# GpSimd left out of the weight splits and the decay products, with another set of thread ranks, in a two-model float32 forward pass

## The chip, the cores and the metric

The kernel runs on one core of one Trainium2 chip. The metric is the time of one execution in microseconds, as the device measures it; lower is better. The engines are named as in the profile: PE (TensorE), DVE (VectorE), ACT (ScalarE), POOL (GpSimd), SP (which issues the DMAs).

## The reference, cut to what matters

256 tokens of width 1024 go through three layers, in float32. Each layer mixes tokens, adds the result to the residual, and runs a gated feed-forward network of width 2816. The three mixers are a linear attention with per-channel decay (and attention over a memory of 256 tokens), a sparse attention in blocks (compressed, selected and windowed keys, and the memory again), and an attention with forget gates beside a pooling branch, with 16 meta tokens ahead of the sequence. The linear attention is the part of which the argument speaks most:

```python
b = jnp.cumsum(gc, axis=2)
o_inter = jnp.einsum('bhtd,bhde->bhte', qc * jnp.exp(b), S)
decay = jnp.exp(jnp.where(causal, b[:, :, :, None, :] - b[:, :, None, :, :], -jnp.inf))
attn = jnp.einsum('bhtd,bhsd,bhtsd->bhts', qc, kc, decay)
o = o_inter + jnp.einsum('bhts,bhse->bhte', attn, vc)
```

The weights are 149 MB in float32 and are read once.

## The kernel before, in words

**Products.** Every large product is made of three TensorE products of rounded parts: the weight is split into `whi` (rounded, made on ScalarE in `_cuts`) and `wlo` (the rest, a subtraction in `_rest`), the activation into `xh` and `xl`, and `mm3` issues hi by hi, lo by hi and hi by lo into one bank of PSUM (`acc`, four of them). One such triple of 128x256 is called a dense triple here. Weights come in chunks of 1 MB into two buffers `wraw`; a chunk is two pieces of 1024 columns, and each piece is one cast to `whi` and one subtraction to `wlo`, 280 pieces in all. A buffer is loaded again when both subtractions of its chunk are done.

**Small work.** Everything else uses four further banks (`att`): scores, transposes, the small products of the three mixers, and the sums for the norms.

**The linear attention.** `expo` makes, for each half `tt` of the tokens and each pair of heads `f`, the tile of exponentials `ge` (8 spans of 128), multiplies it by the queries into `gqe`, and then in place by the keys (128x896 each: these are the decays of the title). At the last span it makes `gkx` or `gqx`, which link the two halves. `levels` then issues, for each half, the products `gqe` by `ge` for spans of 16, 8, 4, 2 and 1 tokens (level 2 to 6, shape 32x16), the diagonal `gq` by `gk` (level 7, 32x32), the two widest spans (64x64 and 32x32), and after both halves `gqx` by `gkx`. `near_pairs` takes the levels out of the banks with predicated copies into `near`, two for each level, and copies `near` into the attention matrix `gat`. `out_rows` multiplies `gat` with the values `gv`. Meanwhile the program's main thread issues dense triples.

**What sets the order.** The kernel is written as threads (generators) that each yield the next operation. `Sched.run` plans with estimated durations and picks the next operation among all threads; the order in which it picks is the order in which the instructions stand in each engine's queue. Of the operations that could start, it takes the one with the lowest sum of estimated start and rank:

```python
                cost, it = min(((self.cost(th, o), o) for o in it.alts), key=lambda c: c[0] + c[1].dur)
                rank = th.prio if it.eng != "P" or th.prio != 9 or self.credit >= 0 else -12
                rank = cost + NEAR * rank
```

The ranks are in the table `PRIO`, by the thread's name. An operation may have alternatives on several engines (written with `|`), of which the planner takes the one with the earliest estimated end. `credit` is an account of how dense TensorE's work has been; when it falls below zero, the main thread's dense triples go first. `RATIO` says how much a dense stretch adds to it, and `LIMIT` is its ceiling. The waits between engines follow from the order in which the instructions were picked: an instruction that touches a tile waits for those before it, in the order of picking, that touched the same part of it in a way that conflicts.

Nearly every instruction of ScalarE, VectorE and GpSimd carries line 335 in the profile, the place where a picked operation is issued, and the matmuls line 516; tiles tell them apart.

Of the kernel before, what the change touches and what calls it, by code (L numbers as in the profile page):

```python
# [153 lines left out]
class Thread:  # L154
    def __init__(self, gen, prio, t, n):
# [2 lines left out]

LNEXP, EXPTANH, SILU = "natural_log_exp_and_others", "exp_and_others", "silu_and_others"
TABLES = {"Exp": (LNEXP, EXPTANH), "Ln": (LNEXP,), "Silu": (SILU,), "Tanh": (EXPTANH,)}  # L160
LOAD, TICK, RATIO, LIMIT, WARM, SWITCH = 1.3, 3.4133, 1.4792, 0.7664, 12, 0.13
NEAR = 0.00100

PRIO = {"_cuts": -18.58, "_load": 1.02, "_loads": -36.85, "_rest": -3.82, "add_residual": -13.55,
        "both_norms": -19.45, "ck_load": -13.23, "ck_loads": -83.76, "coefs": 59.38, "compress": -19.77,
        "consts": 24.44, "decay": -37.28, "evacuate": 6.42, "expo": -55.79, "few_loads": 48.21, "forget": -38.18,
        "fox_chain": -4.22, "fox_pair": 5.05, "proj_few": 10.05, "fox_head": 2.42, "gains": 32.58, "gate": 23.42,
        "gating": -11.27, "head_norm": -20.5, "heads_of": -2.08, "hidden": 7.95, "late_loads": -16.69,
        "levels": 7.47, "mem_chain": -63.57, "mem_head": -11.75, "meta_probs": 1.9, "meta_rows": 0.62,
        "meta_values": -15.47, "mix": -47.97, "near_pairs": -10.15, "nsa_chain": -4.61, "out_rows": -68.21,  # L170
        "output": -6.62, "pads": 18.74, "pooling": -11.72, "rows_done": 28.61, "rstd_rows": -52.41,
        "scale_few": -6.07, "scale_out": -25.81, "scale_tok": -70.73, "selection": 91.16, "silu": 15.66,
        "smalls": 30.82, "square_sum": -6.06, "squares": 39.11, "stack_k": -9.03, "stack_q": 22.34, "swap": 33.71,
        "tile_parts": -14.4, "up": -47.17, "values": -19.21, "warm": -9.83, ("square_sum", 3): 31.92,
        ("square_sum", 5): 13.26}
HOP = {"P": 0.24, "V": 0.14, "S": 0.16, "G": 0.29, "D": 0.24}


# [222 lines left out]
class Weights:  # L401


    def __init__(self, sch, plan, dram, dma, V, S, G, raw, hi, lo):
        self.sch, self.plan, self.dram, self.dma, self.V, self.S, self.G = sch, plan, dram, dma, V, S, G
        self.raw, self.hi, self.lo = raw, hi, lo
        self.chunks, tiles = [], [[] for _ in plan]
        for n, ts in _chunks(plan):
            parts = [Piece() for _ in range(0, n, PIECE)]
            for i, _, o, m in ts:  # L410
                parts[o // PIECE].uses += 1
                tiles[i].append((parts[o // PIECE], o % PIECE, m))
            self.chunks.append((n, parts, Ev()))
        self.blocks = list(zip(plan, tiles))[::-1]
# [38 lines left out]

    def _rest(self, p, raw, o, m, left):
        p.lo = yield self.lo
        parts = p.lo[:, :m], raw[:, o:o + m], p.hi[:, :m].bitcast(FT)
        yield self.V.tensor_sub(*parts) | self.G.tensor_sub(*parts)
        self.sch.set(p.ev)
        left[0] -= 1
        if not left[0]:  # L460
            self.sch.give(self.raw, raw)
# [21 lines left out]
def body(tc, io):  # L483
# [40 lines left out]
    def tr(*calls):  # L524

        def fn():
            for o, a, b in calls:
# [12 lines left out]
    m0 = mem.rearrange("p a b -> p (a b)")  # L540
    gfn, rmeta = base.tile([128, KD], FT, name="gfn"), base.tile([16, 1], FT, name="rmeta")
    tinys = [base.tile([128, 32], FT, name=f"tiny{i}") for i in range(2)]
    W = Weights(sch, _plan(), io["w"], dma, V, S, G, slots(base, 2, [128, CHUNK], "wraw"),
                slots(base, NP, [128, PIECE], "whi", FR), slots(base, NP, [128, PIECE], "wlo", FR))
    rco = base.tile([128, 10], FT, name="rco")
    rsq = base.tile([128, 10], FT, name="rsq")
# [419 lines left out]
    def main():  # L966
# [25 lines left out]
        with ExitStack() as stack:  # L992
# [84 lines left out]
            def expo(tt, f, out):  # L1077
                c = slice(tt * 128, tt * 128 + 128)
                yield la_ev, gr_ev
                et = yield e_  # L1080
                e = et.rearrange("p (a b) -> p a b", a=8)
                qe = yield qes
                for half in range(2):
                    bank = yield att
                    a0 = 128 * tt + 512 * half
                    yield pe(*[(bank, w[:, tt, f * 128:f * 128 + 128], gr[:, a0:a0 + 512], i == 0, i == 1)
                               for i, w in enumerate((lh, ll))])
                    yield S.activation(et[:, half * 512:half * 512 + 512], bank, AF.Exp, scale=1.0 / 16.0)
                    give(att, bank)
                yield q_ev[f], k_ev[f]  # L1090
                l0 = 1 - tt
                yield V.tensor_mul(qe, e[:, l0:l0 + 7], qT[:, f, None, c].to_broadcast([128, 7, 128]))
                ke = e[:, l0:l0 + 7]
                parts = ke, ke, kT[:, f, None, c].to_broadcast([128, 7, 128])
                yield V.tensor_mul(*parts) | G.tensor_mul(*parts)
                if tt == 0:
                    yield V.tensor_mul(kx[:, f, :], e[:, 0], kT[:, f, c])
                else:
                    yield V.tensor_mul(qx[:, f, :], e[:, 7], qT[:, f, c])
                kx_ev[tt, f] = Ev()  # L1100
                sch.set(kx_ev[tt, f])
                out.append((et, qe, ke))
# [973 lines left out]
```

## Time and profile before

| | before |
|---|---|
| three timed runs | 923.35, 929.02, 929.19 us |
| median | 929.02 us |
| the profiled execution | 923.24 us, its span 921.5 us |
| busy, PE / DVE / ACT / POOL | 899.9 / 717.0 / 493.2 / 90.4 us |
| mean granted TensorE clock | 0.989 |

The profiled execution is one more execution beside the timed runs. Its span goes from the first to the last instruction. Matmuls overlap each other in the records, so the distance between the starts of two says more than the duration of one.

### The profile page before, as it was taken

The page shows a single profiled execution, that of the slowest core. Times are in us where ns is not written, and L with a number is a line of the kernel's source. Part 1 is how long each engine was busy: PE and PEld are TensorE (multiplying, and loading weights), DVE is VectorE, ACT ScalarE, POOL GpSimd, SP SyncE. Part 2 cuts the span into 40 slices and gives each one's busy share as a digit, 9 for nine tenths or more (in the row PEclk, how much of TensorE's full clock was granted, in tenths as well). Part 3 has the DMA queues.
Part 4 walks back from the last instruction along what each step waited for, and adds up shares of the span by engine and source line. Part 5 has one row for each costly group of instructions (what it writes and reads, how often), then busy time and mean ns, then how long its engine had stood idle before and what let it go on. Part 6 is the DMA issues. An engine that isn't in the chain of part 4 may idle for free.

```text
span 921.5 us, 19560 instructions
## 1 busy us (share of the span) xinstructions
PE 899.9 (98%) x7967; PEld 864.7 (94%) x7967; DVE 717.0 (78%) x1492; ACT 493.2 (54%) x854; POOL 90.4 (10%) x116
## 2 busy tenths in 40 slices
PE   8988999999999999999999999999999999999998
PEld 7877999999999996989999999999889999999998
DVE  7776588999987687986899999867688777777552
ACT  5644556555554544875565555545666554444431
POOL 3211001000000012300200000112352100000000
PEclk9977999999999999999999999999999999999999
DMA  7721535555555566233445555555323355555651
GB/s 268 265 70 70 183 138 169 198 183 193 200 202 184 190 239 238 90 138 96 180 184 186 200 206 188 184 186 206 131 93 128 127 182 205 185 187 194 217 209 64
DMA packets 26668, 160.19 MB, mean 174 GB/s; under 512 B 3242, under 2 KB 5674, under 8 KB 8530
## 3 DMA queue, kind: packets, MB, share of 16 engines
q1 hardware_dynamic: 26578, 158.94, 48.5%
q8 instruction: 63, 1.03, 0.4%
q14 instruction: 27, 0.22, 0.1%
HBM read 157.62 MB, written 1.05 MB: 172 GB/s over the span
## 4 chain that ended last, share of the span: by engine, by line
PE 86%; DVE 10%; DMA 2%; issue 1%; ACT 0%; SPq 0%; DVEq 0%; ACTq 0%
PE acc L516 76%; PE att L516 8%; DVE wlo L335 4%; PE att L528 2%; DVE xl L335 2%; DMA ck<-in_w_cv_dram 1%; DVE x L335 1%; DVE sum L335 1%; DMA ck<-in_w_ck_dram 1%; DMA mem<-in_w_dram 0%; DVE xh L335 0%; DVE gqx L335 0%; DVE ge L335 0%; DVE gqe L335 0%; DVE near L335 0%
## 5 line engine op out<-in xcount | busy, mean ns | idle before, releaser
L335 ACT CAST whi<-wraw 128x1024 fp32r<-128x1024 f32 x280 | 294.4, 1052 | 319.5 <-PE acc L516 305.0
L335 DVE TENSOR_TENSOR wlo<-wraw,whi 128x1024 fp32r<-128x1024 f32 x279 | 345.2, 1238 | 103.8 <-ACT whi L335 102.9
L516 PE MATMUL acc<-xh,whi 128*128 128x256 f32 (+1 forms) x1440 | 408.2, 283 | 0.1
L516 PE MATMUL acc<-xh,wlo 128*128 128x256 f32 (+1 forms) x1440 | 400.9, 278 | 2.0 <-DVE wlo L335 2.0
L516 PE MATMUL acc<-xl,whi 128*128 128x256 f32 (+1 forms) x1440 | 401.0, 278 | 1.4 <-DVE xl L335 1.3
L516 PEld LDWEIGHTS acc<-xh,whi 128*128 128x128 f32 x1440 | 271.4, 189 | 6.5 <-issue 4.2
L516 PEld LDWEIGHTS acc<-xl,whi 128*128 128x128 f32 x1440 | 271.9, 189 | 2.6 <-DVE xl L335 2.2
L516 PEld LDWEIGHTS acc<-xh,wlo 128*128 128x128 f32 x1440 | 271.4, 188 | 2.8 <-DVE wlo L335 2.8
L516 PE MATMUL acc<-hh,whi 128*128 128x256 f32 x528 | 146.0, 276 | 0.0
L516 PE MATMUL acc<-hl,whi 128*128 128x256 f32 x528 | 145.7, 276 | 0.0
L516 PE MATMUL acc<-hh,wlo 128*128 128x256 f32 x528 | 145.7, 276 | 0.0
L516 PEld LDWEIGHTS acc<-hh,whi 128*128 128x128 f32 x528 | 99.1, 188 | 0.0
L516 PEld LDWEIGHTS acc<-hl,whi 128*128 128x128 f32 x528 | 99.1, 188 | 0.0
L516 PEld LDWEIGHTS acc<-hh,wlo 128*128 128x128 f32 x528 | 99.1, 188 | 0.0
L335 POOL TENSOR_TENSOR sum<-sum,sqt 128x256 f32<-128x256 f32 x27 | 28.9, 1070 | 477.5 <-ACT sqt L335 469.0
L516 PE MATMUL acc<-ch,whi 128*128 128x256 f32 x192 | 55.3, 288 | 0.0
L516 PE MATMUL acc<-cl,whi 128*128 128x256 f32 x192 | 53.1, 277 | 0.0
L516 PE MATMUL acc<-ch,wlo 128*128 128x256 f32 x192 | 53.1, 277 | 0.0
L335 DVE SCALAR_TENSOR_TENSOR fa<-pad,vec,fa 128x256 f32<-128x256 f32 x88 | 41.7, 478 | 0.0
L335 DVE TENSOR_TENSOR fb<-acc,nb 128x256 f32<-128x256 f32 x66 | 28.0, 424 | 12.4 <-PE acc L516 9.6
L516 PEld LDWEIGHTS acc<-ch,whi 128*128 128x128 f32 x192 | 36.1, 188 | 0.7 <-issue 0.4
L335 DVE TENSOR_TENSOR x<-acc,x 128x256 f32<-128x256 f32 x64 | 26.3, 418 | 12.9 <-PE acc L516 12.6
(337 smaller groups left out, 1044.5 us busy)
## 6 DMA issues: line engine op xcount, KB each, us to landing
wraw<-in_w_dram SPq DMA_DIRECT2D x140, 1024.0 KB, 4.8
ck<-in_w_ck_dram SPq DMA_DIRECT2D x4, 512.0 KB, 5.6
ck<-in_w_cv_dram SPq DMA_DIRECT2D x4, 512.0 KB, 5.5
x<-in_x_dram SPq DMA_DIRECT2D x4, 256.0 KB, 6.0
mem<-in_w_dram SPq DMA_DIRECT2D x4, 256.0 KB, 4.6
mem<-in_mem_dram SPq DMA_DIRECT2D x1, 1024.0 KB, 6.9
out_dram<-sqt SPq DMA_DIRECT2D x8, 128.0 KB, 2.1
ge<-in_gcst_dram SPq DMA_DIRECT2D x2, 288.0 KB, 7.5
```

What stands on the lines that cost most here:

```text
L335: op_ = Op(self.name, d, lambda: f(out, *a, **k), table=table)
L516: r = P.matmul(o, a, b, start=s, stop=e)
L528: r = P.transpose(o, a, b)
```

## The change

Two lines lose their alternative on GpSimd: the subtraction to `wlo` and the product of the exponentials with the keys. GpSimd keeps small operations (sums of squares, powers, bias tiles, scalings of 128x128 and the like). All ranks of `PRIO` are other numbers, as are `RATIO`, `LIMIT` and `NEAR`. What is computed is the same. Cut to its core:

```diff
-LOAD, TICK, RATIO, LIMIT, WARM, SWITCH = 1.3, 3.4133, 1.4792, 0.7664, 12, 0.13
-NEAR = 0.00100
+LOAD, TICK, RATIO, LIMIT, WARM, SWITCH = 1.3, 3.4133, 1.3862, 1.2333, 12, 0.13
+NEAR = 0.00101
...
-PRIO = {"_cuts": -18.58, "_load": 1.02, "_loads": -36.85, "_rest": -3.82, "add_residual": -13.55,
+PRIO = {"_cuts": -12.17, "_load": 1.37, "_loads": -52.68, "_rest": -5.17, "add_residual": -7.56,
...
-        parts = p.lo[:, :m], raw[:, o:o + m], p.hi[:, :m].bitcast(FT)
-        yield self.V.tensor_sub(*parts) | self.G.tensor_sub(*parts)
+        yield self.V.tensor_sub(p.lo[:, :m], raw[:, o:o + m], p.hi[:, :m].bitcast(FT))
...
-                parts = ke, ke, kT[:, f, None, c].to_broadcast([128, 7, 128])
-                yield V.tensor_mul(*parts) | G.tensor_mul(*parts)
+                yield V.tensor_mul(ke, ke, kT[:, f, None, c].to_broadcast([128, 7, 128]))
```

What this does to the instructions is seen in the order that the planner made, with and without the change. On TensorE the order is the same through the three feed-forward networks; it differs in the linear attention from the first half's level 5 on, in the sparse attention, and in the third mixer. Of the 280 subtractions to `wlo`, GpSimd has one before and none now, and the products with the keys stand on VectorE before and now. Of the scalings of `np` (the sparse attention's probabilities), GpSimd has two of 128x128 and one of 128x256 before, and five of 128x128 now.

On GpSimd, in the linear attention, before (`nt` and `tiny` are the powers for the norms):

```order
L335 TENSOR_TENSOR sum_90<-sum_90,sqt_86 128x256
L335 TENSOR_TENSOR nt_94<-tiny_64,mhalf 128x2
L335 TENSOR_TENSOR wlo_72<-wraw_66,whi_68 128x1024
L335 TENSOR_TENSOR tiny_98<-tiny_98,mhalf 128x4
L335 TENSOR_TENSOR tiny_99<-tiny_99,mhalf 128x4
```

And now:

```order
L335 TENSOR_TENSOR sum_90<-sum_90,sqt_87 128x256
L335 TENSOR_TENSOR sum_90<-sum_90,sqt_88 128x256
L335 TENSOR_TENSOR sum_90<-sum_90,sqt_86 128x256
L335 TENSOR_TENSOR nt_94<-tiny_64,mhalf 128x2
L335 TENSOR_TENSOR tiny_98<-tiny_98,mhalf 128x4
L335 TENSOR_TENSOR tiny_99<-tiny_99,mhalf 128x4
```

The subtraction is gone, and its neighbours stand as they did.

On VectorE, in the second half of the linear attention, before (from the link `gqx`; `sr` and `mq` are scaled projections, `xl` are the low parts of the memory's activations, `near` the predicated copies):

```order
L335 TENSOR_TENSOR gqx<-ge_132,gq 128x128
L335 TENSOR_TENSOR sr<-acc_113,nb_93 128x256
L335 SCALAR_TENSOR_TENSOR xl_81<-mem,vec,xh_80 128x256
L335 SCALAR_TENSOR_TENSOR mq<-acc_114,nb_93 128x256
L335 SCALAR_TENSOR_TENSOR xl_81<-mem,vec,xh_80 128x256 x7
L335 COPY_PREDICATED near<-gc,att_117 128x2x16
L335 COPY_PREDICATED near<-gc,att_116 128x2x16
L335 TENSOR_TENSOR wlo_73<-wraw_65,whi_69 128x1024
L335 COPY_PREDICATED near<-gc,att_117 128x4x8
L335 COPY_PREDICATED near<-gc,att_116 128x4x8
```

And now:

```order
L335 TENSOR_TENSOR gqx<-ge_132,gq 128x128
L335 TENSOR_TENSOR sr<-acc_113,nb_93 128x256
L335 SCALAR_TENSOR_TENSOR mq<-acc_114,nb_93 128x256
L335 SCALAR_TENSOR_TENSOR xl_81<-mem,vec,xh_80 128x256 x8
L335 TENSOR_TENSOR wlo_72<-wraw_66,whi_68 128x1024
L335 TENSOR_TENSOR wlo_73<-wraw_65,whi_69 128x1024
L335 COPY_PREDICATED near<-gc,att_119 128x2x16
L335 COPY_PREDICATED near<-gc,att_116 128x2x16
```

Two subtractions to `wlo` now stand ahead of the first predicated copy, where one stood between the first pair and the second.

On TensorE, in the same half, with the engines that each waits for, before (16 products of level 7 `gq` by `gk`, of which the first two stand here, then the widest spans):

```order
L516 MATMUL acc3_115<-xh0_78,wlo3_74 128x256
L516 MATMUL att1_117<-gq_135,gk_136 32x32 [waits DVE_49]
L516 MATMUL att0_116<-gq_135,gk_136 32x32
...
L516 MATMUL att1_117<-gqe0_343,ge1_133 64x64 [waits DVE_49]
L516 MATMUL att0_116<-gqe0_343,ge1_133 64x64 [waits DVE_49]
L516 MATMUL att1_117<-gqe1_344,ge0_132 64x64 [waits DMAHW0_49]
```

And now:

```order
L515 MATMUL acc3_115<-xh0_78,wlo3_74 128x256
L515 MATMUL att3_119<-gq_135,gk_136 32x32
L515 MATMUL att0_116<-gq_135,gk_136 32x32
...
L515 MATMUL att3_119<-gqe0_343,ge1_133 64x64
L515 MATMUL att0_116<-gqe0_343,ge1_133 64x64
L515 MATMUL att3_119<-gqe1_344,ge0_132 64x64 [waits DMAHW0_49]
```

The products stand without a wait for VectorE now, since the predicated copies were picked after all of them. The first wait for VectorE that is left in this half for a result of the predicated copies stands later, at the product of `gat` with `gv` for the second half, after nine dense matmuls, the four products of the first half and nine dense matmuls more. In the first half, level 5 waited for the first predicated copy of level 4 and now waits for the two of level 2; a dense triple that stood ahead of it stands behind it.

In the third mixer, for one pair of heads, the sums `hns1` for the head norms, two products `fk` by `fq` and the transposes of `fp3` and `fp0` now stand on TensorE with no dense triple between them, with four waits for VectorE and one for ScalarE; before, a dense triple stood between the sums and the products, one transpose stood behind them, and of the four waits two were for VectorE and two for ScalarE.

The count of places on TensorE where one matmul's tile shape (rows by columns of the array) differs from the next one's is 22 before and 17 now in the linear attention, 34 and 32 in the sparse attention, 56 and 53 in the third mixer.

## Rows read from the trace of the kernel before

**Rows 1.** Windows: busy us (count) of PE, PEld, DVE, ACT, POOL, granted clock, DMA share, GB/s.

```profile
44.40:54.60 10.20, 7.41 (x225) 6.04 (x226) 6.83 (x21) 2.50 (x6) 1.91 (x2) 0.75 0.36 130
54.60:64.80 10.20, 10.20 (x103) 9.34 (x104) 7.46 (x19) 5.86 (x13) 1.77 (x1) 0.75 0.00 0
64.80:75.10 10.30, 5.18 (x229) 4.31 (x219) 8.40 (x26) 2.33 (x6) 1.47 (x1) 0.75 0.29 105
75.10:127.00 51.90, 51.90 (x356) 48.45 (x355) 34.16 (x74) 30.39 (x69) 2.92 (x2) 0.95 0.35 122
...
150.80:327.00 176.20, 176.20 (x1557) 176.20 (x1556) 147.82 (x254) 94.27 (x130) 1.47 (x2) 1.00 0.54 193
327.00:370.00 43.00, 39.94 (x346) 33.47 (x345) 35.53 (x80) 19.74 (x32) 8.35 (x10) 1.00 0.69 241
370.00:460.70 90.70, 89.74 (x744) 82.19 (x743) 73.23 (x231) 61.63 (x160) 12.42 (x15) 1.00 0.34 123
...
638.00:718.00 80.00, 79.20 (x691) 71.12 (x692) 61.08 (x211) 50.86 (x121) 30.04 (x49) 1.00 0.33 119
```

**Rows 2.** Waits of PE for one tile, whole span: total us, times, longest us.

```profile
PE att L516 <- DVE near L335: 7.9, 4, 4.1
```

**Rows 3.** Timeline of PE, first half of the linear attention: start, duration, idle before.

```profile
44.38 0.28 PE L516 MATMUL acc<-xh,wlo 128*128 128x256 f32 x1
44.58 1.07 PE L516 MATMUL att<-gqe,ge 64*32 64x16 f32 x96
...
48.14 0.39 PE L516 MATMUL att<-gqe,ge 64*32 64x16 f32 x32 [1.94 <-DVE near L335]
...
49.94 0.58 PE L516 MATMUL att<-gqe,ge 64*32 64x16 f32 x32 [0.85 <-DVE near L335]
```

**Rows 4.** Timeline of PE, second half, to the last of its products.

```profile
64.63 1.07 PE L516 MATMUL att<-gqe,ge 64*32 64x16 f32 x96
...
72.06 0.52 PE L516 MATMUL att<-gq,gk 64*32 64x32 f32 x32 [4.10 <-DVE near L335]
73.60 1.18 PE L516 MATMUL att<-gqe,ge 64*64 64x64 f32 x24 [1.02 <-DVE near L335]
...
76.24 0.41 PE L516 MATMUL acc<-xl,whi 128*128 128x256 f32 x1
...
81.28 0.37 PE L516 MATMUL acc<-xh,whi 128*128 128x256 f32 x1
```

**Rows 5.** Timeline of DVE over both halves, and in the sparse attention.

```profile
36.52 0.28 DVE L335 TENSOR_TENSOR gkx<-ge,gk 128x128 f32<-128x128 f32 x1
...
63.95 2.67 DVE L335 TENSOR_TENSOR gqx<-ge,gq 128x128 f32<-128x128 f32 x2
66.65 0.42 DVE L335 TENSOR_TENSOR sr<-acc,nb 128x256 f32<-128x256 f32 x1
...
67.72 2.85 DVE L335 SCALAR_TENSOR_TENSOR xl<-mem,vec,xh 128x256 fp32r<-128x256 f32 x7
70.49 0.28 DVE L335 COPY_PREDICATED near<-gc,att 128x32 f32<-128x32 uint8 x2
70.69 1.22 DVE L335 TENSOR_TENSOR wlo<-wraw,whi 128x1024 fp32r<-128x1024 f32 x1
...
75.08 1.22 DVE L335 COPY gat<-near 32x64 f32<-32x64 f32 x8
76.32 0.65 DVE L335 COPY gat<-att 64x128 f32<-64x128 f32 x3
...
385.37 0.37 DVE L335 TENSOR_SCALAR np<-np,tiny 128x128 f32<-128x128 f32 x1
...
387.25 0.28 DVE L335 TENSOR_SCALAR np<-np,tiny 128x128 f32<-128x128 f32 x1
```

**Rows 6.** Timeline of POOL.

```profile
63.03 3.24 POOL L335 TENSOR_TENSOR wlo<-wraw,whi 128x1024 fp32r<-128x1024 f32 x1 [10.59 <-ACT whi L335]
...
385.30 0.60 POOL L335 TENSOR_SCALAR np<-np,tiny 128x128 f32<-128x128 f32 x1 [10.45 <-DVE tiny L335]
```

More of the change, by code (lines that the diff above doesn't have):

```diff
@@ L160 @@
 TABLES = {"Exp": (LNEXP, EXPTANH), "Ln": (LNEXP,), "Silu": (SILU,), "Tanh": (EXPTANH,)}
-LOAD, TICK, RATIO, LIMIT, WARM, SWITCH = 1.3, 3.4133, 1.4792, 0.7664, 12, 0.13
-NEAR = 0.00100
-PRIO = {"_cuts": -18.58, "_load": 1.02, "_loads": -36.85, "_rest": -3.82, "add_residual": -13.55,
[L165 to L175, printed above, removed]
@@ new lines @@
+LOAD, TICK, RATIO, LIMIT, WARM, SWITCH = 1.3, 3.4133, 1.3862, 1.2333, 12, 0.13
+NEAR = 0.00101
+PRIO = {"_cuts": -12.17, "_load": 1.37, "_loads": -52.68, "_rest": -5.17, "add_residual": -7.56,
+        "both_norms": -33.22, "ck_load": -15.44, "ck_loads": -83.53, "coefs": 40.79, "compress": -19.2,
+        "consts": 36.87, "decay": -34.57, "evacuate": 4.06, "expo": -64.07, "few_loads": 45.42, "forget": -21.91,
+        "fox_chain": -3.12, "fox_pair": -7.57, "proj_few": 19.88, "fox_head": 8.36, "gains": 38.33, "gate": 50.08,
+        "gating": -14.29, "head_norm": -36.58, "heads_of": -11.63, "hidden": -0.76, "late_loads": -3.72,
+        "levels": 0.78, "mem_chain": -69.93, "mem_head": -9.86, "meta_probs": -21.08, "meta_rows": -15.24,
+        "meta_values": 4.27, "mix": -62.03, "near_pairs": 2.77, "nsa_chain": -9.52, "out_rows": -71.71,
+        "output": -17.96, "pads": 9.38, "pooling": -17.95, "rows_done": 25.04, "rstd_rows": -64.13,
+        "scale_few": -10.36, "scale_out": -20.17, "scale_tok": -36.67, "selection": 77.08, "silu": 5.66,
+        "smalls": 40.36, "square_sum": -10.21, "squares": 50.38, "stack_k": -3.54, "stack_q": 16.96, "swap": 48.72,
+        "tile_parts": -15.56, "up": -32.71, "values": -13.07, "warm": -5.76, ("square_sum", 3): 28.89,
+        ("square_sum", 5): 15.72}
@@ L401, with __init__ @@
 class Weights:
-    def __init__(self, sch, plan, dram, dma, V, S, G, raw, hi, lo):
-        self.sch, self.plan, self.dram, self.dma, self.V, self.S, self.G = sch, plan, dram, dma, V, S, G
+    def __init__(self, sch, plan, dram, dma, V, S, raw, hi, lo):
+        self.sch, self.plan, self.dram, self.dma, self.V, self.S = sch, plan, dram, dma, V, S
         self.raw, self.hi, self.lo = raw, hi, lo
@@ L542, in body @@
     tinys = [base.tile([128, 32], FT, name=f"tiny{i}") for i in range(2)]
-    W = Weights(sch, _plan(), io["w"], dma, V, S, G, slots(base, 2, [128, CHUNK], "wraw"),
+    W = Weights(sch, _plan(), io["w"], dma, V, S, slots(base, 2, [128, CHUNK], "wraw"),
                 slots(base, NP, [128, PIECE], "whi", FR), slots(base, NP, [128, PIECE], "wlo", FR))
```

## The prediction

> **What bounds the kernel now.** I read the windows first, then TensorE's waits, then the timelines at the places where those waits stand. TensorE is busy for 899.9 of 921.5 us, so time can only come from its idle stretches, from its slow stretches, and from matmuls that take less. In a feed-forward network it is busy without a gap: 1557 dense matmuls in 176.20 us, 0.113 us each, at full clock [rows 1]. The change leaves TensorE's order there as it was, and about 530 us of the span lie in such stretches; I count them at nothing. The sparse attention idles for 3.06 us in its first 43.00 us and 0.96 in the next 90.70, the third mixer for 0.80 of 80.00 [rows 1]: little is to be had there. What is left is the linear attention. From 44.4 to 75.1 us the granted clock is 0.75, half of the time at the lower level, 1.2 GHz instead of 2.4, and in the next 51.9 us it is 0.95 [rows 1]; a dense matmul takes 0.41 us at 76.24 where it takes 0.28 at 44.38 [rows 3, 4]. There TensorE also waits four times for the predicated copies `near`, 7.9 us in all, the longest 4.1 [rows 2]: 1.94 and 0.85 in the first half [rows 3], 4.10 and 1.02 in the second [rows 4].
>
> **The GpSimd alternatives themselves.** Only one subtraction of 280 moves, and no decay product does. On GpSimd it took 3.24 us [rows 6]; on VectorE one takes 1.22 [rows 5]. In its time, from 63.03 on, VectorE's two products `gqx` took 2.67 us, where one of the same shape, the counterpart `gkx` at 36.52, took 0.28 [rows 5]. So VectorE loses 2.67 less 0.56, 2.1 us, beside the subtraction, and 1.22 by taking it over. By themselves these edits are worth at most 0.9 us, and only as far as TensorE waits for VectorE.
>
> **Second half of the linear attention.** Before, from the first level product at 64.63 to the dense matmul behind the last `gv` product at 81.28 are 16.65 us, of which 5.12 are the two waits [rows 4]. The levels stood behind copies that VectorE reached late: `gqx` took 2.67, and from 66.65 to 70.49 came `sr`, `mq` and eight `xl`, 3.84 us, then a subtraction of 1.22 between the copies [rows 5]. Now the products carry no wait for VectorE; the wait has moved to the product of `gat` and `gv`, behind nine dense matmuls, four products and nine dense matmuls. Does VectorE get there in time? From 63.95: two `gqx` at 0.28, 0.56; `sr` to `xl`, 3.84; two subtractions at 1.22, 2.44; twelve predicated copies at 0.14, 1.68; eight `gat` from `near`, 1.22; three from the bank, 0.65 [rows 5]. The sum is 10.39, which ends at 74.3. TensorE has 16.65 less 5.12, 11.53 us of work in the stretch, and three dense triples more, nine matmuls at 0.113, 1.0 us: it would be through at 77.2 without a wait, and the second half's `gv` products, which need `gat`, are the last of it; 2.9 us are left for them behind VectorE's end. So I hold the waits to be gone. Where they go, those three triples come out of later work, so the gain is up to 5.12 us. It is less if the lower clock lasts as long as before and is now spent on dense matmuls: at half speed 5.12 us of waits turn into 5.12 us of work worth 2.56 at full speed. Between 2.56 and 5.12 I take 4.0. Below 2.56 lies a late VectorE: each microsecond beyond the 2.9 us of slack (74.3 against 77.2) costs one, and the second subtraction can itself wait for ScalarE's `whi`, on which nothing here has a price. I let that reach to a gain of nothing.
>
> **First half.** Level 5 now waits for two copies of level 2 instead of one of level 4, and one triple that stood ahead of it stands behind it. The waits are 1.94 and 0.85 [rows 3], so the gain lies between 2.79 and, if the missing triple (0.34 us) is added to the wait, -0.3. With the earlier copy and the later triple pulling opposite ways I take half, 1.4.
>
> **Tile shapes.** From a dense matmul at 44.38 to products of another shape at 44.58 are 0.20 us [rows 3], against 0.113 in a dense run [rows 1]: about 0.09 for a change of shape. There are ten fewer (22, 34 and 56 become 17, 32 and 53), 0.9 us. It is nothing if the change hides under weight loads.
>
> **Sparse attention and third mixer.** All 4.8 us of idle there are the most that could go, and some of it waits for DMAs that the change doesn't touch. Against that, the third mixer has a stretch with five waits and no dense triple between them. Every further wait is new; from a gain of 1 to a loss of 3 I take a loss of 0.5. GpSimd also gets five scalings of `np` of 128x128 for two and a wider one. At 385.30 such a scaling took 0.60 us [rows 6], and VectorE's own beside it 0.37, against 0.28 at 387.25 [rows 5]: 0.09 lost for each, 0.3 for three more, on an engine with slack; it is inside the 0.5. The Trainium skill, SBUF — State Buffer (two separate sides), would make that dearer: the port pair that GpSimd and VectorE share is an exclusive lock, and the loser fully blocks. By that rule three more scalings could hold VectorE for up to 1.8 us instead of 0.3, an estimate from the row's 0.60; this row shows a slowing and no full block, and I keep the row's price.
>
> **Sum.** 923.24 - 4.0 - 1.4 - 0.9 + 0.5 = 917.4 us, against the profiled execution. That execution lies with the fastest of the three timed runs (923.35); the other two are 5.9 us longer, so their median is 929.02. The trace doesn't show what they had more; a further stretch at the lower clock would fit, but that is an inference. I forecast a time like the profiled one's.
>
> **The rivals.**
>
> *The clock stays up.* If TensorE no longer idles in the second half, the clock may not fall there. Before, it was 0.95 over the 51.9 us from 75.1 [rows 1], 5.2 us at half speed, which cost 2.6; with all of the 5.12 gained instead of 4.0 this gives 917.4 - 2.6 - 1.1 = 913.7. For it: the lower clock stands around the waits. Against: the window from 54.6 to 64.8 is at 0.75 too, with TensorE busy for all of its 10.20 us [rows 1], so a busy engine is not at once a fast one. The Trainium skill, TensorE: Matmul & The Clock Gate (What's actually happening), speaks for this rival: the default state is throttled, and activity releases it. The row of the busy window neither confirms nor refutes it.
>
> *The runs keep their longer time.* Whatever lengthened two of three runs by 5.9 us stays, and the median falls among such runs: 917.4 + 5.9 = 923.3. Against it: a stretch with fewer waits has fewer occasions.
>
> *What is gained is given back.* The linear attention's gap moves to the `gat` products, or later small products come late by as much. Then the kernel takes what it took, 923 to 929; I take 924. For it: VectorE's own work grows by 10 instructions and ScalarE's falls by as many, and both feed the same products.
>
> *Slower.* The third mixer's stretch with five waits makes TensorE idle as the linear attention does, and the clock falls with it. The price is the linear attention's own: some 4 us of idle, half of the 7.9 [rows 2], and a stretch like that from 44.4 to 75.1, where half of 30.7 us at half speed cost 7.7 [rows 1], 11.7 together. With only 2.56 and 0.9 gained elsewhere that is 923.24 + 11.7 - 3.5 = 931.4. It decides from the point where those waits and their clock cost more than the 6.3 us that I add up as gains. Against it: before, the third mixer had waits of the same kinds and idled for 0.80 us at a clock of 1.00 [rows 1].
>
> **How the numbers follow.** A measurement of this kernel can tell about 1% from no change, so faster means below 919.7 and slower above 938.3. The forecast has 0.45, of which 0.40 lies below 919.7; the clock that stays up 0.13; the longer runs 0.22; nothing gained 0.10; slower than before 0.10, of which half passes 938.3 if the runs' 5.9 us come on top. Faster is 0.40 + 0.13 = 0.53, slower 0.05, the same the remaining 0.42. The forecast's own range is 914.5 to 920.5. The whole range reaches down to 911, the clock that stays up with the first half's waits gone too, and up to 926, past the longer runs and most of nothing gained; the slower rival and part of nothing gained are left out above, with 0.05 below.
>
> **What would show it.** In the changed trace: no wait for `near` ahead of the second half's widest spans, and none over 1 us at `gv` by `gat`; `gqx` at 0.28 each; dense matmuls resuming with three triples more done, some 4 us ahead of the old row; the granted clock from 75 to 127 us at 0.95 (forecast) or 1.00 (first rival); idle of at most some 2 us from 638 to 718. The feed-forward networks at 176.2 us each. The prediction is wrong if VectorE reaches the `gat` copies late, if the idle time moves behind the linear attention, or if a longer stretch at the lower clock takes back what the waits gave.

## The result, and the profile after

The changed kernel takes 920.1 us (median of 20 runs, 912.91 to 928.9), the kernel before in the same sitting 929.87 (20 runs). The ratio is 0.9881 with a 95% interval of 0.9854 to 0.9908: about 1.2% faster. The profiled execution went from 923.24 to 917.79 us, its span from 921.46 to 915.92. Executions that the comparison sets aside as disturbed are in the medians and not in the ratios. The ratio stands for 11 us; between runs that are alike in one respect, the number of networks that took longer (next section), the difference is 8 us.

First the windows of the changed kernel (busy us and count of PE, PEld, DVE, ACT, POOL, then the granted clock, DMA share, GB/s), which answer to [rows 1]:

```profile
44.40:54.60 10.20, 7.83 (x239) 6.68 (x239) 6.91 (x28) 1.96 (x6) 2.13 (x2) 0.80 0.38 137
54.60:64.80 10.20, 10.20 (x187) 9.53 (x187) 8.89 (x20) 7.51 (x17) 0.00 (x0) 0.87 0.01 2
64.80:75.10 10.30, 9.29 (x130) 8.44 (x130) 7.99 (x32) 2.80 (x11) 0.00 (x0) 0.67 0.32 103
75.10:127.00 51.90, 51.90 (x376) 48.94 (x375) 36.47 (x71) 29.41 (x58) 1.98 (x2) 1.00 0.41 143
...
638.00:718.00 80.00, 79.35 (x678) 72.19 (x678) 60.34 (x209) 49.01 (x115) 27.62 (x47) 1.00 0.30 107
```

From 64.8 to 75.1 TensorE is busy for 9.29 us where it was for 5.18, and its granted clock there is 0.67, below the 0.75 of before; behind 75.1 it is full, where it had been 0.95. The third mixer idles as little as before.

TensorE's waits for `near` in the changed kernel (total, times, longest), against 7.9 in [rows 2]:

```profile
PE att L515 <- DVE near L335: 2.1, 2, 1.8
```

Both of them stand in the first half, where a third wait, for a sum of the norms, is new:

```profile
47.60 0.48 PE L515 MATMUL att<-gqe,ge 64*32 64x16 f32 x32 [1.75 <-DVE near L335]
48.99 0.48 PE L515 MATMUL att<-gqe,ge 64*32 64x16 f32 x32 [0.35 <-DVE near L335]
50.28 0.81 PE L515 MATMUL att<-ones,sum 128*128 128x1 f32 x4 [0.26 <-DVE sum L335]
```

The timeline of TensorE in the second half of the linear attention, beside [rows 4]:

```profile
63.26 1.35 PE L515 MATMUL att<-gqe,ge 64*32 64x16 f32 x128
...
65.96 0.32 PE L515 MATMUL att<-gq,gk 64*32 64x32 f32 x13
67.28 0.36 PE L515 MATMUL att<-gq,gk 64*32 64x32 f32 x19 [1.01 <-issue]
...
70.09 0.41 PE L515 MATMUL acc<-xl,whi 128*128 128x256 f32 x1
...
74.98 0.38 PE L515 MATMUL att<-gv,gat 128*128 128x128 f32 x2
...
76.68 0.36 PE L515 MATMUL acc<-xh,whi 128*128 128x256 f32 x1
```

From the first level product to the dense matmul behind the last `gv` product it is 13.42 us instead of 16.65, with nine dense matmuls more in it. The waits of 4.10 and 1.02 are gone; in their place stands a gap of 1.01 that no semaphore in the trace releases (the last section has what goes with it). The dense matmul at 70.09 takes 0.41: the clock fell here too. The timeline of VectorE, beside [rows 5]:

```profile
62.78 0.48 DVE L335 TENSOR_TENSOR gqx<-ge,gq 128x128 f32<-128x128 f32 x2
...
67.02 2.35 DVE L335 TENSOR_TENSOR wlo<-wraw,whi 128x1024 fp32r<-128x1024 f32 x2
69.29 1.56 DVE L335 COPY_PREDICATED near<-gc,att 128x32 f32<-128x32 uint8 x12
...
71.99 0.65 DVE L335 COPY gat<-att 64x128 f32<-64x128 f32 x3
74.23 0.22 DVE L335 COPY gat<-att 32x64 f32<-32x64 f32 x1 [1.59 <-ACT gat L335]
```

And of ScalarE:

```profile
73.74 0.28 ACT L335 ACTIVATE lt<-att 128x128 f32<-128x128 f32 x1 [2.73 <-PE att L515]
...
74.01 0.18 ACT L335 COPY gat<-att 32x64 f32<-32x64 f32 x1
```

Without GpSimd beside it, the two `gqx` take 0.48 us instead of 2.67. VectorE is through with three of its four copies from the bank at 72.64; the last waits for a copy of ScalarE, which stands behind an operation that waited for TensorE itself. It ends at 74.45, half a microsecond before the product that needs it.

Where the span went, by stages (us). A mixer's stage ends where its last output product on `ch` or `cl` starts, a network's where its last product on `hh` or `hl` starts:

| | linear attention | network 1 | sparse attention | network 2 | third mixer | network 3 | span |
|---|---|---|---|---|---|---|---|
| before | 141.79 | 181.79 | 128.04 | 182.73 | 101.70 | 181.83 | 921.46 |
| changed | 136.08 | 181.78 | 128.89 | 182.66 | 101.16 | 181.77 | 915.92 |

### The profile page after: what moved, and what is told of

The parts are those of the page before. It is cut to its first block, busy times and chain, and to the rows that moved or that the text cites. A ratio compares the mean times of both kernels' runs of the same rounds, so it can differ in the third digit from the quotient of the medians.

```text
span 915.9 us, 19557 instructions
## 1 busy us (share of the span) xinstructions
PE 898.7 (98%) x7967; PEld 865.1 (94%) x7967; DVE 716.4 (78%) x1502; ACT 489.8 (53%) x844; POOL 86.8 (9%) x116
## 4 chain that ended last, share of the span: by engine, by line
PE 88%; DVE 9%; DMA 1%; issue 1%; ACT 0%; SPq 0%; DVEq 0%; ACTq 0%
PE acc L515 78%; PE att L515 8%; DVE wlo L335 4%; PE att L527 2%; DVE xl L335 2%; DVE x L335 1%; DMA ck<-in_w_cv_dram 1%; DVE sum L335 1%; DMA x<-in_x_dram 1%; DVE xh L335 0%; DVE qst L335 0%; SPq L499 0%; ACT whi L335 0%; DVE flat L335 0%; DVE fp L335 0%
## 5 line engine op out<-in xcount | busy, mean ns | idle before, releaser
L515 PEld LDWEIGHTS acc<-cl,whi 128*128 128x128 f32 x192 | 36.1, 188 | 0.3
```

Of the source, the lines that this page charges most:

```text
L515: r = P.matmul(o, a, b, start=s, stop=e)
```

## The experiments

Each was timed beside the kernel before (12 runs; six in the tenth); the diffs are cut to their core. Single executions differ by several us for reasons that lie in the networks: one of them may take some 6 us longer (the last section). A ratio therefore mixes in how many such long networks its runs happened to have. They can be told apart, since each run's granted clock is on record. I take off 0.92 us for each 0.001 by which it lies under 1 (an estimate: that share of a span of 920 us). Then the 20 runs of the changed kernel fall into three groups: eight from 908.5 to 910.1, eight from 915.2 to 917.3, four from 922.0 to 924.1. Their measured means are 915.1, 922.2 and 928.5 us. Each traced execution lies where the number of long networks in its trace, none to two, puts it. The kernel before has no clocks on record in that sitting, but its times part as well: three at 922.55 to 924.43, fourteen at 928.67 to 932.97, three at 935.23 to 938.14, with means of 923.4, 930.2 and 936.7. Group by group the changed kernel takes 8 us less; the other 3 us of the ratio come from how many runs each group got. A table at the end of this section has the first group of each experiment where the groups lie at least 2.4 us apart.

The traces are compared by one stretch: from the first level product to the last output product of the linear attention, which holds the same 1002 matmuls in every kernel. Its row has the length, TensorE's busy time and, behind POOL, the granted clock. Before, and in the changed kernel:

```profile
44.58:141.79 97.21, 89.30 (x1002) 82.87 (x1002) 69.24 (x161) 49.87 (x107) 9.60 (x8) 0.89 0.32 112
```

```profile
44.78:136.08 91.30, 87.92 (x1003) 82.42 (x1002) 68.78 (x167) 48.02 (x101) 5.46 (x7) 0.93 0.35 120
```

It is 5.9 us shorter: idle time fell from 7.91 to 3.38 us, busy time by 1.4 with the better clock. My theory was A, that the place of the predicated copies does it; the rivals were B, that GpSimd's edit does, and C, the later mixers.

**1. The edit alone.**

```diff
-        yield self.V.tensor_sub(*parts) | self.G.tensor_sub(*parts)
+        yield self.V.tensor_sub(*parts)
...
-                yield V.tensor_mul(*parts) | G.tensor_mul(*parts)
+                yield V.tensor_mul(*parts)
```

> The kernel before with the two GpSimd alternatives taken out and all ranks as they were. Two theories. A, the order: the time came from the place of the predicated copies `near` in the order of picking, which decides whether TensorE waits for them. B, the edit: it came from GpSimd's subtraction, beside which `gqx` took 2.67 us instead of 0.56. Under A this kernel keeps a wait for `near` ahead of the second half's level 7: the copies still come before it, behind one subtraction. By the rows of before it is 4.10 less the 2.1 us that `gqx` gains, about 2; the wait of 1.02 ahead of the 64x64 products is gone, the first half's 2.8 us stay. That is some 2 to 3 us, a profiled time near 921 and a ratio of 0.997. Under B both waits of the second half go and the time is that of the changed kernel, 917.8, ratio 0.990.

Measured: 927.07 against 928.31, ratio 0.998 (0.9944 to 1.0016). Its stretch, and its waits for `near`:

```profile
44.90:139.26 94.36, 88.91 (x1003) 82.11 (x1003) 67.54 (x159) 49.89 (x110) 6.40 (x7) 0.91 0.34 115
```

```profile
PE att L516 <- DVE near L335: 4.3, 3, 2.0
```

2.9 us shorter, with 4.3 us of waits for `near` left, the longest 2.0, as A had it. B as the whole cause is out. TensorE's order is that of before, matmul by matmul; idle time fell by 2.5 us, busy time by 0.4.

**2. The new ranks in the linear attention only.** The tables are swapped between the networks:

```diff
+            if self.at["P"] > SWAPS[self.stage + 1]:
+                self.stage += 1
+                RATIO, LIMIT, NEAR, PRIO = TABS[self.stage]
```

> The changed kernel's ranks and its edit up to the first feed-forward network, and from there on the ranks of before, so that the sparse attention and the third mixer stand in the order of before. If the gain is made in the linear attention, the first network ends as early as in the changed kernel, 5.7 us before the kernel before, and nothing of that is lost or added later: a profiled time of about 917.5, ratio 0.990. Rival C, the later mixers: if these carried the gain, the time is near 923 and the ratio 1.000.

Measured: 921.73, ratio 0.9925 (0.9885 to 0.9966); the profiled execution took 921.95 and not 917.5, with a second network of 188.04 us. The stretch:

```profile
44.82:134.10 89.28, 86.41 (x1002) 81.02 (x1002) 68.79 (x167) 47.99 (x102) 5.45 (x7) 0.94 0.34 123
```

The gain is there without the later mixers. It is also 2 us shorter than in the changed kernel's trace, where the same instructions stand in this stretch up to its very end: busy time is 1.5 us less, at a clock of 0.94 instead of 0.93. So one order can differ by 2 us from one execution to the next, 1.5 of it in busy time at another clock.

**3. The copies last, nothing else.**

```diff
                 h = slice(2 * e, 2 * e + 2)
+                yield evs[0]
                 for lv in range(2, 8):
```

> The kernel before, ranks and GpSimd alternatives as they were, but the predicated copies of each half may start only when the half's last level product (64x64) has been issued. Theory A: the four waits for `near`, 7.9 us, vanish without any other rank or the edit; some come back as a wait for `gat` ahead of the `gv` products and as dense matmuls at the lower clock, so a gain of 4 to 6 us is expected, profiled 917 to 919, ratio about 0.993. Theory B: with GpSimd's subtraction still there VectorE is 2.1 us late, so a wait of 3 us or more for `gat` takes the place of the old one and the time stays at 921 to 923.

Measured: 925.73, ratio 0.9992 (0.9957 to 1.0027): theory A, which had 0.993, fails. (The profiled execution took 932.9 us, with two long networks.) The waits of TensorE show why:

```profile
PE att L516 <- DVE sum L335: 3.6, 4, 2.1
PE att L516 <- issue: 1.8, 2, 1.0
...
PE att L516 <- DVE ge L335: 1.1, 1, 1.1
```

None is for `near`; 2.1 us came back for the sums of the norms, 1.1 for `ge` and 1.0 with no releaser. On VectorE, GpSimd's subtraction now fell beside the products with the keys, two of which took 2.08 us in the changed kernel:

```profile
61.70 4.29 DVE L335 TENSOR_TENSOR ge<-ge,gk 128x896 f32<-128x896 f32 x2
```

The second of these products ended at 65.99. GpSimd's subtraction ended at 65.04:

```profile
62.30 2.75 POOL L335 TENSOR_TENSOR wlo<-wraw,whi 128x1024 fp32r<-128x1024 f32 x1 [10.20 <-ACT whi L335]
```

The stretch was 93.25 us in this one trace, 4 less than before; the timed runs don't show those 4. Their mean granted clock was 0.9902, that of the kernel before 0.9901, in the first experiment 0.9922 and in the second 0.9945. How much of the 4 us another execution keeps is open.

**4. The changed kernel with the old rank of the copies.**

```diff
-"near_pairs": 2.77
+"near_pairs": -10.15
```

> The changed kernel with one rank put back, that of `near_pairs` (-10.15 in place of 2.77), so that the copies are picked ahead of the second half's level 7 again. Theory A: a wait for `near` comes back there. VectorE now reaches the first pair of copies at 67.0, and with the subtraction behind them and the second pair it is 68.8, against 66.0 where TensorE could start: 2.8 us of wait where the changed kernel has a gap of 1.0. A loss of about 1.8 us, profiled 919.5. Theory B: no change, 917.8. With other orders behind it in the linear attention, either may be off by 1.

Measured: 919.01, ratio 0.994 (0.9904 to 0.9975). Waits for `near` came back:

```profile
PE att L515 <- DVE near L335: 3.6, 3, 1.8
```

The one that came back is 1.5 us long, ahead of level 7, where A had 2.8; and since it stands in place of the gap of 1.0, idle time in the stretch grew by 0.5 alone, from 3.4 to 3.9. The stretch of this trace was 89.86 us long, at a clock of 0.94, and shorter than the changed kernel's 91.30. In the timed runs without a long network it takes 917.2 us, 2 more than the changed kernel: a loss of A's size, a quarter of the gain, made in part of the clock (mean 0.992 against 0.9936).

After this I took up D: GpSimd's subtraction delays what VectorE does beside it, the place of the copies decides whether TensorE waits there, and either alone only moves the wait; and E: the time follows the clock alone.

**5. Both: the edit and the copies last, old ranks** (the diffs of 1 and 3 together).

> The kernel before without the two GpSimd alternatives and with the predicated copies of each half only behind its last level product; ranks as before. Theory D, both: GpSimd's subtraction delays whatever VectorE does beside it by 2 us and more, and the copies' place decides whether TensorE waits there; each alone only moves the wait. Then this kernel loses both: no wait for `near` and none for `ge` ahead of the second half's levels, from the first level product to the end of the first mixer's output products about 92 us against 97.2 before and 93.3 with the copies last alone, ratio 0.994 to 0.996. Theory E, the clock: what counts is how long TensorE is left at the lower level, and waits matter only through it. Then the time follows the mean granted clock of the runs, half a us for each us at the lower level, and at the clock of the kernel before (0.990) the ratio is 0.999 whatever the waits.

Measured: 922.14 against 923.92, ratio 0.9944 (0.9908 to 0.998).

```profile
44.56:134.28 89.72, 86.22 (x1002) 80.04 (x1002) 67.98 (x163) 49.17 (x106) 5.48 (x7) 0.94 0.35 121
```

```profile
PE att L516 <- DVE sum L335: 3.9, 5, 2.1
...
PE att L516 <- DVE gat L335: 1.2, 1, 1.2
```

7.5 us came off the stretch, 4.4 of it idle and 3.1 busy time at the better clock. The wait of 2.1 for the sums stayed, as in the third experiment, and one of 1.2 for `gat` is new. Only both changes together are clear of no change in the timed runs; without a long network they take 916.3 us, 7 less than the kernel before. But D's "either alone only moves the wait" is not shown. In single traces the first change took 2.9 us off the stretch and the second 4.0, together nearly what both do, and the intervals of their ratios don't exclude a gain of 2 or 3 us for each. E said no gain at the old clock; the clock itself rose (0.9945 over the runs), so the two go together.

**6. The new ranks in the later mixers only** (the swap of 2 the other way round, with the edit).

> The kernel before without the alternatives, with its own ranks up to the first feed-forward network and the changed kernel's ranks behind it: the sparse attention and the third mixer stand in the changed order, the linear attention in that of the first experiment. Theory D: the third mixer gains 0.5 us (101.2 for 101.7), the sparse attention nothing; beside the first experiment that is no difference to be measured, ratio 0.997. Rival C, the later mixers: a ratio of 0.994 or less.

Measured: 924.45, ratio 0.995 (0.991 to 0.999), between D's 0.997 and C's 0.994. The linear attention ended at 139.28, as in the first experiment (139.26). The third mixer took 101.15 us; in the new order it took 101.15 to 101.19 in all traces, in the old one 101.70 to 102.44. The sparse attention took 127.26; over all traces it is 126.05 to 128.89 in eight of the new order, on average 127.2, and 127.79 to 129.39 in five of the old, on average 128.5. So the later mixers' order gives 0.5 us for sure and some 1.8 on average. D had 0.5; C, that they carry the gain, stays out, since the second experiment has most of it without them.

**7 and 10. VectorE delayed ahead of the copies**, in the changed kernel, by 30 and by 8 memsets:

```diff
+                    if tt == 1 and e == 0 and lv == 2:
+                        op.fn = lambda: ([nc.vector.memset(near[:, 1, h], 0.0) for _ in range(30)], fn())[1]
```

> The changed kernel with 30 small memsets on VectorE (they clear a part of `near` that is zero anyway) ahead of the second half's first predicated copy, some 2 to 3 us more for VectorE and nothing else moved. The prediction's own slack was 2.9 us, by which nothing would change. Theory D reads the trace of the changed kernel: the last `gat` copy ended 0.5 us ahead of the product that needs it, so all but 0.5 us of the delay comes back as a wait for `gat`: 1.5 to 2.5 us slower than the changed kernel, ratio to the kernel before 0.991 in place of 0.988. Theory E: as much again if the clock falls with that wait.

> The seventh experiment with 8 memsets in place of 30, by its trace (5.67 us for 30) 1.5 us more for VectorE. With 0.5 us of slack the wait for `gat` is 1.0 us where the level products run at the lower clock, and some 2.6 where they run at the full one, since TensorE then comes sooner. Ratio 0.990 to 0.992 if each us of delay costs one; more, if the clock falls for longer with it. With the prediction's 2.9 us of slack it is 0.988, as in the changed kernel.

Measured: with 30 memsets 925.36, ratio 0.9998 (0.9964 to 1.0032); with 8, 915.39, ratio 0.9891 (0.9861 to 0.9922). The 30 took longer than I had thought, and the wait came at `gat`:

```profile
69.36 5.67 DVE L1117 MEMSET near<- 128x64 f32 x30
```

```profile
PE att L515 <- DVE gat L335: 6.8, 1, 6.8
```

With 8 memsets (1.45 us) TensorE waited 0.81 us at that place, and its stretch was 89.96 us. What slack there is depends on the clock. From the first level product to the point where TensorE needs this `gat`, in the changed kernel and with 8 and 30 memsets (waits for `gat` left out), it goes through the same 257 matmuls:

```profile
63.26:74.98 11.72, 10.71 (x257) 9.83 (x257) 9.53 (x37) 4.34 (x15) 0.00 (x0) 0.71 0.28 92
```

```profile
62.37:72.91 10.54, 9.39 (x257) 8.52 (x256) 9.84 (x42) 3.64 (x10) 0.00 (x0) 0.84 0.28 100
```

```profile
63.27:71.86 8.59, 7.82 (x257) 6.94 (x256) 7.55 (x27) 3.12 (x7) 0.00 (x0) 1.00 0.28 97
```

11.72 us at a clock of 0.71, 10.54 at 0.84, 8.59 at 1.00. VectorE's own copies ended 2.3 us before that point in the changed kernel's trace. At 0.84 a delay of 1.45 cost 0.81, so 0.6 was free; at 1.00 a delay of 5.67 cost 6.8, so nothing was. A TensorE that keeps its clock meets VectorE's end sooner. Without a long network, the delay of 5.67 us leaves 922.2 us, 7 of the 8 us lost, with a mean clock back at 0.990. The six runs with 8 memsets had no long network, which is why their ratio is so low; their mean is 915.8, level with the changed kernel's 915.1.

**8. The alternatives back, under the new ranks.** The diff of 1 reversed, in the changed kernel; some `gv` and transposing products stand elsewhere with it.

> The changed kernel's ranks with both GpSimd alternatives put back. The planner then gives GpSimd one subtraction again, in the second half of the linear attention. Theory A, the order alone: no difference from the changed kernel, ratio 0.988. Theory D: VectorE loses 2 us or more beside that subtraction (`gqx` or `xl` takes so much longer), gains 1.2 by not doing it, and the products of `gat`, which stand earlier now, wait 1 to 2 us: ratio 0.990.

Measured: 924.31, ratio 0.998 (0.9948 to 1.0012). The planner gave GpSimd one subtraction, and it met the products with the keys again:

```profile
61.17 2.46 POOL L335 TENSOR_TENSOR wlo<-wraw,whi 128x1024 fp32r<-128x1024 f32 x1 [9.53 <-ACT whi L335]
```

```profile
60.30 4.28 DVE L335 TENSOR_TENSOR ge<-ge,gk 128x896 f32<-128x896 f32 x2
```

The second product ended at 64.58, 0.95 us behind the end of the subtraction at 63.63, where such a product takes 1.04 by itself: it made next to no headway until GpSimd was through. TensorE waited 1.6 us for `ge`, and 2.58 of a gap without a releaser stood in level 7. Its ratio is not clear of 1, but that is in part the long networks: the three mixers together took 367.7 us in this trace (before 371.5, changed 366.1), and the two shortest runs, 918.22 and 919.47, lie 4 us under the first group of the kernel before. So undoing the edit costs some 4 of the 8 us by these runs: D's direction, and about twice its size. How much of it the gap of 2.58 makes is open.

**9. The best parts together**: the fifth experiment's linear attention, the changed kernel's later mixers.

> The kernel before up to the first feed-forward network, without the alternatives and with the copies behind each half's last level product (the order of the fifth experiment), and behind it the order of the changed kernel. Theory D: the first mixer's output products end at 134.3 us as in the fifth experiment (136.1 in the changed kernel's trace), the third mixer takes 101.2, so a profiled time of 913 to 916 with the networks at 181.8, 182.7 and 181.8, and a ratio of 0.988 to 0.991: level with the changed kernel or a little faster. If only the changed kernel's own ranks in the linear attention make its gain, 0.994.

Measured: 920.22 against 924.88, ratio 0.9953 (0.9921 to 0.9985). The profiled execution took 914.84 us, with the stages as expected. The ratio is that of runs of which nine in twelve had one or two long networks; group by group they took 914.4, 920.9 and 926.2 us, level with the changed kernel or 1 to 2 us less, as D had it.

**11. GpSimd work beside VectorE, nothing else moved.**

```diff
+                if tt == 1 and f == 0:
+                    op.fn = lambda: ([nc.gpsimd.tensor_mul(z, z, qe[:, 0]) for _ in range(4)], fn())[1]
```

> The changed kernel with four more multiplications of 128x128 on GpSimd (they write zeros over zeros in `near`), which start when VectorE has made the first `gqe` of the second half; on TensorE and VectorE nothing is moved. Theory D: the two products `ge` beside them take some 4.3 us in place of 2.08, as in the third and eighth experiments, TensorE waits 1.0 to 1.6 us for them ahead of the levels, and the rest of VectorE's chain ends 2.2 us later, so a wait of 1 to 2 us for `gat` as well: 2 to 4 us slower than the changed kernel, ratio 0.990 to 0.993. Theory A, the order alone: 0.988.

Measured: 922.09, ratio 0.9935 (0.9902 to 0.9969), as if it were slower than the changed kernel by the size expected. But the trace doesn't show the way there that I gave:

```profile
59.36 4.45 POOL L1096 TENSOR_TENSOR near<-near,gqe 128x128 f32<-128x128 f32 x4 [7.24 <-DVE gqe L335]
```

```profile
60.20 2.62 DVE L335 TENSOR_TENSOR ge<-ge,gk 128x896 f32<-128x896 f32 x2
62.75 0.74 DVE L335 TENSOR_TENSOR gqx<-ge,gq 128x128 f32<-128x128 f32 x2
```

4.45 us of GpSimd cost VectorE 0.5 us in `ge` and 0.3 in `gqx`, not 2.2; the wait for `gat` was 1.3 us, and the stretch of this trace 89.64 us. Here both engines slowed each other: three of the four short operations took 1.2 us and the last 0.6, and a product `ge` 1.35 instead of 1.08, where the subtraction is one long operation. The price of GpSimd's subtraction isn't that of any GpSimd work. Nor do the timed runs show a loss: nine or more of the twelve had long networks, and the seven that lie at 915.0 to 918.0 in the reckoning above took 922.2 us on average, as the changed kernel's middle group did. Their ratio is the number of long networks.

**All by the first group.** Runs without a long network, where the groups part (for the kernel before, the sitting of the experiments 5 to 8). The groups were made after the fact, from few runs in several sittings; a difference of 1 us says nothing here.

| | runs without a long network | their mean, us |
|---|---|---|
| before | 20 of 35 | 923.0 |
| changed | 8 of 20 | 915.1 |
| 1, the edit alone | 5 of 12 | 920.6 |
| 2, new ranks in the linear attention | 5 of 12 | 916.7 |
| 4, old rank of the copies | 6 of 12 | 917.2 |
| 5, the edit, copies last | 4 of 12 | 916.3 |
| 6, new ranks in the later mixers | 5 of 12 | 918.4 |
| 7, 30 memsets | 6 of 12 | 922.2 |
| 9, 5 and the new ranks later | 3 of 12 | 914.4 |
| 10, 8 memsets | 6 of 6 | 915.8 |

## Why the prediction was right

**The time.** 917.4 was forecast for an execution like the profiled one, with a range of 914.5 to 920.5; the median of 920.1 lies in it, in part by luck. Runs without a long network took 915.1 us, 2.3 less than forecast, since the clock kept up further; runs with one took 922.2, above the range. The median fell between the two because eight of twenty had none. At equal numbers of long networks the gain is 8 us, where 5.8 were forecast.

**What bounds.** Right: the three networks take the same in both traces, and the gain was made in the linear attention (the table above).

**Second half, 4.0.** Measured by the same working: 16.65 less 13.42, and 1.0 for the nine matmuls, 4.25 us. The mechanism is the one forecast: the waits of 5.12 gone, part of it given back, here as a gap of 1.01 and dense matmuls at 0.41 us. Two things were missing on the way. The gap of about 1 us seems to have been there before, hidden under the wait (last section), so that it could not be gained. And the slack of 2.9 us left the clock out: VectorE's own work took 9.86 us (62.78 to 72.64), where I had 10.39 with the last copy, which waits for ScalarE; TensorE was at its products 11.7 us behind the first level product, not 12.6. In this execution 2.3 us were left for VectorE; at the full clock, where TensorE takes 8.6, none are (the seventh experiment).

**First half, 1.4.** From the first level product of the first half to that of the second it was 20.05 us and is 18.48: 1.57, with 60 dense matmuls in both. The two windows, before and now:

```profile
44.58:64.63 20.05, 17.26 (x292) 15.15 (x291) 13.94 (x39) 8.00 (x19) 3.33 (x3) 0.74 0.17 62
```

```profile
44.78:63.26 18.48, 16.11 (x291) 14.45 (x290) 13.88 (x43) 7.55 (x16) 1.75 (x2) 0.82 0.19 68
```

The number came out by luck. The 1.4 were to be half of the waits, but idle time only fell from 2.79 to 2.37 us (1.75 and 0.35 for `near`, 0.26 for the sum); the other 1.15 are busy time at a clock of 0.82 instead of 0.74.

**Tile shapes 0.9, later mixers -0.5.** Together a gain of 0.4; in the two profiled executions it is a loss of 0.2: behind the last `gv` product the linear attention takes 60.54 and 59.43, 1.0 of which are the nine matmuls; the third mixer gains 0.54, the sparse attention loses 0.85. That last number is the execution's and not the order's. In the changed kernel's trace the clock fell for a while in the sparse attention, as it did there in no other of the 13 traces:

```profile
350.00:370.00 20.00, 18.07 (x138) 14.07 (x137) 12.89 (x38) 11.38 (x29) 1.80 (x2) 0.91 0.41 153
```

At 0.91 these 20 us can have lost 1.8. Over all traces the sparse attention gains 1.3 (the sixth experiment). The loss of 0.5 that I took for the later mixers was a gain of 1 to 2; whether fewer changes of tile shape made it wasn't tried.

**The edit, at most 0.9.** Too small: alone it took 2.9 us off the stretch of its trace (the first experiment), and under the new ranks its undoing cost some 4 of the 8 us (the eighth). I set 2.1 us of VectorE against 1.22. But the delay hits `ge` or `gqx`, ahead of the levels and of everything behind them, while the subtraction that VectorE takes over stands later, where some time was free. The prediction's row of the two `gqx` had the price, 2.2 us; I netted it where only the first place counts. For the scalings of `np` I kept a slowing of 0.09 us and no full block; beside the subtraction it is as good as a block: what VectorE had begun ended 0.15 to 0.95 us behind GpSimd's end in three traces.

**The rivals.** That the clock stays up came partly true: behind 75.1 us it is 1.00, and over the timed runs its mean is 0.9936 against 0.990 for the kernel before (in the experiments' sittings), which is 3.3 us of the span at full clock. The profiled pair, at 0.991 against 0.989, gained 5.5; the timed runs gained 8 at equal numbers of long networks, and 9.8 by the median. That the runs keep their longer time came true as well: 917.79 is the profiled time and 920.1 the median, for both kernels have runs with long networks. My inference on them, one more stretch at the lower clock, is not borne out (next but one section). In the profiled execution nothing was given back at `gat`. The slower rival didn't show: the third mixer idles for 0.65 us from 638 to 718.

## What to carry to other kernels

An engine that helps out can cost more than it takes: weigh a subtraction on GpSimd by what VectorE does beside it and who waits for that, not by VectorE's sum. Part of a wait that is removed can turn up at the next late thing, so try two causes alone and together. When a chain's end and its reader lie close, count the slack at the full clock, since the lower clock can hide the reader's wait. Where single runs fall into groups, compare group with group: a ratio of all runs can be moved by how many fell into each.

## What the runs showed of the hardware

A network takes one of two times. In 13 traces 32 of the 39 networks took 181.6 to 182.7 us, and seven took 188.0 to 188.6, at a granted clock of 1.00. The same 40 us of the first network before, and in the third experiment:

```profile
180.00:220.00 40.00, 40.00 (x356) 40.00 (x355) 36.50 (x67) 21.67 (x30) 0.00 (x0) 1.00 0.56 197
```

```profile
180.00:220.00 40.00, 40.00 (x342) 40.00 (x342) 35.22 (x65) 20.45 (x28) 0.00 (x0) 1.00 0.56 189
```

356 matmuls against 342 without a gap: 0.112 and 0.117 us each, and so through all or nearly all of such a network. Each long network adds 5.4 to 6.8 us, which is the size of the 5.9 us between the runs shown ahead of the prediction. It struck each of the three networks in some trace, and neither the order nor the granted clock shows it. That the longer runs of the kernel before are this is inferred from the size and from the groups of the timed runs; none of them has a trace.

In the stretch compared above, busy time follows the clock: 89.3 us at 0.89, 87.9 at 0.93, 86.4 at 0.94, for the same matmuls. What VectorE does beside GpSimd's subtraction stands nearly still until that is through: `gqx` in the trace of before (2.67 us for 0.48) and `ge` in the third and eighth experiments (4.29 and 4.28 for 2.08). Beside four short operations of GpSimd it only slowed (2.62 for 2.08).

In the second half's level 7 TensorE stopped after 5 or 13 of its 32 products with no releaser, for 0.8 to 1.1 us in six traces, for 2.58 in the eighth experiment, and for 0.2 and 0.5 in the fifth and ninth. The DMA queue that loads instructions, over the whole execution of the changed kernel, and in the windows 64.6 to 66.0 there and 68.0 to 69.1 in the eighth experiment:

```profile
q8 instruction: 63, 1.03, 0.5%
```

```profile
q8 instruction: 1, 0.02, 5.5%
```

```profile
q8 instruction: 1, 0.02, 5.6%
```

In each of the nine traces one such packet ends 1.2 to 1.4 us before TensorE goes on: in the changed kernel it runs from 64.68 to 65.92, and TensorE goes on at 67.28; in the eighth experiment from 68.08 to 69.06, when TensorE had stopped already, and it goes on at 70.37. Before, one ended at 67.52, inside the wait of 4.10 us that began at 67.96; by the same 1.2 to 1.4 us TensorE would not have gone on before some 68.8. That TensorE waits there for its next instructions, after more than a hundred small products in a row, fits all of these; no run changed it, so it is not shown.
